# A two-layer decoder trunk on one core: three matmuls for the half-K products, column sums by ones, other homes for VectorE's work, another pace for the modulation, and the first mixer's K in blocks of 4, 6, 6

## The chip, the cores and the metric

The kernel runs on 1 core of one Trainium2 chip. Its time is device microseconds (us) of one launch; lower is better. TensorE (PE) does the matrix products, with weight loads (PEld) of their own beside them; VectorE (DVE), ScalarE (ACT) and GpSimd (POOL) do the rest; SyncE (SP) issues almost all transfers from device memory (DMA).

## The reference

The input is 256 tokens of 2048 features, in fp32. Layer 0 has a gated linear attention (GLA), layer 1 a softmax attention with forget gates (FoX); each is followed by a gated MLP (FFN) with a causal convolution of width 3. Every sub-layer's input is an RMS norm, scaled and shifted by a modulation that is computed from one conditioning vector `c`. That modulation is a matrix of 2048 by 12288 for each layer, used for a single vector.

```python
cond = jax.nn.silu(c)
for i in range(DEPTH):                      # DEPTH = 2
    mod = (cond @ w_mod[i] + b_mod[i])[:, None, :]
    sh_m, sc_m, g_m, sh_f, sc_f, g_f = jnp.split(mod, 6, axis=-1)
    h = rmsnorm(x, norm_mix[i]) * (1.0 + sc_m) + sh_m
    y = gla_mixer(h, ...) if i % 2 == 0 else fox_mixer(h, ...)
    x = x + (1.0 + g_m) * y
    h = rmsnorm(x, norm_ffn[i]) * (1.0 + sc_f) + sh_f
    x = x + (1.0 + g_f) * conv_ffn(h, ...)
return rmsnorm(x, norm_final)
...
# gla_mixer:  proj = h @ w_in  (q 1024, k 1024, v 2048, r 2048, a 16 columns), then chunked attention, @ w_out
# fox_mixer:  proj = h @ w_in  (q, k, v, og of 2048 each, 16 forget gates), softmax attention, @ w_out
# conv_ffn:   u = h @ w_up (2 x 5632 columns), conv, silu(gate) * val, @ w_down
```

## The kernel before, in words

Activations lie transposed (`xT`: features on the partitions, tokens along the free axis), so K comes in 16 tiles of 128 features. The kernel is written as a queue of work for the Tile layer, whose scheduler then sets the order of the instructions on each engine; `tc.issue_after` pins an instruction behind another.

**Products.** Each fp32 product is done with split operands: a weight tile is rounded to `wh` on ScalarE (`split_w`, line 110) and the remainder `wl` is formed on VectorE (line 111); an activation `h` or `op` is held as a high and a low part side by side. `stream_p` takes pairs of K tiles: one load `w` of 512 KB holds two K tiles of 512 columns and feeds eight (column tile, K tile) products. Each such product is a 512-column matmul of `wh` with both parts of `h` next to each other (line 554) and a 256-column one of `wl` with the high part (line 555). The two halves of the result land in different halves of a PSUM bank, and `gather` adds them while it copies them out: one ScalarE copy and one VectorE add (lines 584, 585), or two VectorE adds where an earlier sum is there (lines 582, 585). `stream_b` makes the token-major products (v, and FoX's q and k) of three 512-column matmuls, `narrow` the 16-column gates of three 256-column ones (lines 614 to 616). After every weight load's products `tick()` runs a share of the waiting background and side work.

**Blocks of K.** Products run over a part of K where the modulation for the rest isn't there yet. GLA's input products take K in `BLOCKS` of 8 and 8 tiles: all columns for the first block, then the modulation's queue is drained, then the second block adds to the first (`fold`, `run`). The first FFN does `FIRST` = 6 groups of its up product over the first 8 K tiles, drains, and then their second halves.

**Modulation.** `mod_tasks` cuts a section (`sc_m`, `sh_m`, ...) into chunks of at most 1024 columns. One task loads part of `w_mod` (`wm`) and multiplies its rows by the conditioning values, adding on VectorE into `acc` (the first row by a tensor-scalar on line 250, the others on line 252). In the start the first four K tiles go through TensorE instead (`direct`, line 246). `finish` sums `acc` over its 128 partitions: eight TensorE transposes (line 265), then eight ScalarE passes with an accumulator (line 274; in the start two VectorE reductions), then the bias. A task's load takes one of the same five ring buffers as the weight loads. `pace["bg"]` is the number of tasks per `tick()`; `set_pace(n)` spreads the tasks that wait over n ticks. Chunks marked `defer` are finished in the next `make_h`.

**Side work.** Convolutions, gates and attention steps wait in `side`, popped at `pace["side"]` per tick. In the FFN a group's four gate and four value convolutions go through it; the down product's operand `op` (`raw_operand`) is made from the activations that they write. `make_h` computes the reciprocal root of each token's mean square (`token_rstd`) and makes `h` tile by tile.

The stages in order: start (modulation of the first block, loading x and its squares), GLA input, GLA output with the first residual, FFN up and down, FoX, FoX output, second FFN.

Of the kernel before, what the change touches and what calls it, by code (L numbers as in the profile page):

```python
# [17 lines left out]
P = 128  # L18
# [22 lines left out]
BLOCKS = (8, 8)  # L41
# [14 lines left out]
N1, N2, N3, N4 = 26, 151, 152, 156  # L56
# [8 lines left out]
def kernel(  # L65
# [151 lines left out]
    def mod_tasks(l, key, f0=0, fn=D, wide=False, direct=0, defer=False):  # L217
# [8 lines left out]
        def chunk(c0, kt, st):  # L226
# [8 lines left out]
            def f():  # L235
# [5 lines left out]
                for j in range(per):  # L241
                    k = kt + j
                    col = cT[:, k:k + 1]
                    if k < direct:
                        for m in range(mn):
                            nc.tensor.matmul(st["p"][:, m:m + 1], wt[:, j, m * P:(m + 1) * P], col,
                                             start=(k == 0 and m == 0), stop=(k == direct - 1), skip_group_check=True)
# [11 lines left out]
            def finish():  # L259
                m0, mn = c0 // P, width // P  # L260
                red = tmp.tile([P, 8], F32, tag="red", name=nm("red"))
                for q0 in range(0, mn, 4):
                    pt = bank2("pt")[:, 0, :] if wide or defer else misc()
                    for m in range(min(4, mn - q0)):
                        nc.tensor.transpose(pt[:, m * P:(m + 1) * P], st["a"][:, (q0 + m) * P:(q0 + m + 1) * P],  # L265
                                            ident)
                    if wide:
                        mq = min(4, mn - q0)
                        nc.vector.tensor_reduce(out=red[:, q0:q0 + mq], in_=pt[:, :mq * P]
                                                .rearrange("p (m k) -> p m k", k=P), axis=AX.X, op=ALU.add)  # L270
                        continue
                    for m in range(min(4, mn - q0)):
                        blk = pt[:, m * P:(m + 1) * P]
                        nc.scalar.activation(blk, blk, AF.Copy, accum_out=red[:, q0 + m:q0 + m + 1])
# [140 lines left out]
    def token_rstd():  # L415
# [10 lines left out]
        for _ in range(3):  # L426
            for i in range(2):
                c1 = slice(i, i + 1)
                nc.vector.tensor_scalar(out=t[:, c1], in0=q[:, c1], scalar1=q[:, c1], scalar2=v[:, c1],
                                        op0=ALU.mult, op1=ALU.mult)  # L430
            for i in range(2):
                c1 = slice(i, i + 1)
                nc.vector.tensor_scalar(out=q[:, c1], in0=t[:, c1], scalar1=1.5, scalar2=q[:, c1],
                                        op0=ALU.subtract, op1=ALU.mult)
# [12 lines left out]
    def make_h(l, kind):  # L447
# [8 lines left out]
        def make(m):  # L456
# [8 lines left out]
            nc.scalar.activation(hi, t, AF.Identity, scale=sc, bias=sh)  # L465
            nc.vector.tensor_scalar(out=t, in0=t, scalar1=sc, scalar2=sh, op0=ALU.mult, op1=ALU.add)
# [77 lines left out]
    def stream_p(kts, c0, rhs, done=None):  # L544


        ps = [bank2().rearrange("p j (s t) -> p j s t", s=2) for _ in range(2)]
        held = []

        def mms(m, k, ws, j, hl):  # L550
            first, last = k == kts[0], k == kts[-1]
            ms = slice(j * 512 + m * P, j * 512 + (m + 1) * P)
            o = ps[m // 2][:, m % 2, :, :]
            nc.tensor.matmul(o, ws[0][:, ms], hl, start=first, stop=False, skip_group_check=True)  # L554
            nc.tensor.matmul(o[:, 0, :], ws[1][:, ms], hl[:, 0, :], start=False, stop=last, skip_group_check=True)  # L555
# [21 lines left out]
        return ps  # L577

    def gather(dst, ps, add=False):

        if add:
            nc.vector.tensor_tensor(out=dst, in0=dst, in1=ps[:, :, 1, :], op=ALU.add)
        else:
            nc.scalar.copy(out=dst, in_=ps[:, :, 1, :])  # L584
        nc.vector.tensor_tensor(out=dst, in0=dst, in1=ps[:, :, 0, :], op=ALU.add)  # L585
# [62 lines left out]
    def gla(l, h):  # L648
# [10 lines left out]
        def fold(key, ps):  # L659
# [12 lines left out]
            for b in range(4):  # L672
                dst = parts[key][:, b, :]
                if new:
                    nc.scalar.copy(out=dst, in_=ps[b // 2][:, b % 2, :])
                else:
                    nc.vector.tensor_tensor(out=dst, in0=dst, in1=ps[b // 2][:, b % 2, :], op=ALU.add)

        def run(key, kts, c0):
# [6 lines left out]
            for g in range(2):  # L686
                ps = stream_p(kts, c0 + g * 512, h)
                for b in range(2):
                    gather(parts[key][:, g * 2 + b, :].rearrange("p (j t) -> p j t", j=2), ps[b], not new)
# [210 lines left out]
    def fox(l, h):  # L900
# [43 lines left out]
        def qk_group(c0, gain, dst):  # L944
# [17 lines left out]
            def fin(hp):  # L962
                def f():
                    pt = misc().rearrange("p (j t) -> p j t", j=2)
                    for j in range(2):
                        hh = hp * 2 + j
                        for tt in range(TT):
                            blk = (tt * 2 + hh // 4) * 4 + hh % 4
                            nc.vector.tensor_scalar(out=tok4[:, blk, :], in0=tok4[:, blk, :],
                                                    scalar1=rs[:, blk:blk + 1], scalar2=None, op0=ALU.mult)  # L970
# [10 lines left out]
        def soft(hd):  # L981
            def f():
# [9 lines left out]
                nc.vector.tensor_scalar(out=s[:, 0:P], in0=p_[:, 0:P], scalar1=cumt[:, 0, hd:hd + 1],  # L992
                                        scalar2=None, op0=ALU.add)
# [310 lines left out]
```

## Time and profile before

| | |
|---|---|
| median of 3 runs | 2592.15 us (2590.53 to 2594.13) |
| profiled execution | 2593.84 us; its span 2592.1 us |
| granted TensorE clock, mean | 0.975 |
| read from device memory | 633.14 MB, 245 GB/s over the span |
| transfers of `w_mod` | 352 of 512 KB, 16 of 1024 KB |

A span is the time from the first instruction to the last. A group's row names line, engine and operation, output and inputs, shapes and count, then total busy time and mean ns of one, then the engine's idle time before and what ended it. A row of the timeline gives start and length. A row of the waits names who waited for whom: us in total, times, longest.

### The profile page before, as it was taken

The page shows a single profiled execution, that of the slowest core. Times are in us where ns is not written, and L with a number is a line of the kernel's source. Part 1 is how long each engine was busy: PE and PEld are TensorE (multiplying, and loading weights), DVE is VectorE, ACT ScalarE, POOL GpSimd, SP SyncE. Part 2 cuts the span into 40 slices and gives each one's busy share as a digit, 9 for nine tenths or more (in the row PEclk, how much of TensorE's full clock was granted, in tenths as well). Part 3 has the DMA queues.
Part 4 walks back from the last instruction along what each step waited for, and adds up shares of the span by engine and source line. Part 5 has one row for each costly group of instructions (what it writes and reads, how often), then busy time and mean ns, then how long its engine had stood idle before and what let it go on. Part 6 is the DMA issues. An engine that isn't in the chain of part 4 may idle for free.

```text
span 2592.1 us, 36814 instructions
## 1 busy us (share of the span) xinstructions
PE 2486.6 (96%) x13738; PEld 2139.2 (83%) x13738; DVE 2010.2 (78%) x2784; ACT 1288.2 (50%) x1964; POOL 18.1 (1%) x35
## 2 busy tenths in 40 slices
PE   6999998899999999899999999999899999999998
PEld 6887887788888888788888888778788888888887
DVE  7877988888789999877587888877877777767554
ACT  2447353445555565443454555543655555565332
POOL 0000000000000000000000000100000000000000
PEclk7999998899999999999999999999999999999999
DMA  8896877789567888898589988768577777765653
GB/s 335 276 311 218 294 235 255 247 293 324 178 186 259 295 295 295 269 305 299 178 267 307 305 269 229 215 228 267 171 221 229 226 224 225 223 196 195 191 189 116
DMA packets 267727, 637.67 MB, mean 246 GB/s; under 512 B 23449, under 2 KB 24459, under 8 KB 267164
## 3 DMA queue, kind: packets, MB, share of 16 engines
q1 hardware_dynamic: 267160, 635.17, 75.3%
q8 instruction: 108, 1.77, 0.3%
q14 instruction: 71, 0.58, 0.1%
q10 hardware_dynamic: 388, 0.15, 0.0%
HBM read 633.14 MB, written 2.10 MB: 245 GB/s over the span
## 4 chain that ended last, share of the span: by engine, by line
PE 72%; DVE 12%; DMA 10%; issue 3%; ACT 3%; DVEq 0%; SPq 0%; ACTq 0%
PE pa L554 38%; PE pa L555 19%; DMA wm<-in_w_mod_dram 7%; DVE wl L111 4%; PE pa L601 4%; PE pa L599 4%; PE pa L600 4%; DVE acc L252 3%; ACT wh L110 1%; DVE xT L624 1%; DMA w<-in_ffn_w_down_dram 1%; DMA w<-in_gla_w_in_dram 1%; DMA w<-in_ffn_w_up_dram 0%; PE pm L411 0%; PE pm L265 0%
## 5 line engine op out<-in xcount | busy, mean ns | idle before, releaser
L110 ACT CAST wh<-w 128x1024 fp32r<-128x1024 f32 x819 | 856.2, 1049 | 986.5 <-PE pa L554 429.5
L111 DVE TENSOR_TENSOR wl<-w,wh 128x1024 fp32r<-128x1024 f32 x819 | 994.4, 1218 | 368.0 <-ACT wh L110 361.4
L554 PE MATMUL pa<-h,wh 128*128 128x512 f32 x3584 | 1264.4, 399 | 15.9 <-DVE h L467 7.8
L555 PE MATMUL pa<-h,wl 128*128 128x256 f32 x3584 | 992.8, 282 | 6.7 <-DVE wl L111 6.6
L554 PEld LDWEIGHTS pa<-h,wh 128*128 128x128 f32 x3584 | 671.4, 189 | 169.3 <-ACT h L465 8.1
L555 PEld LDWEIGHTS pa<-h,wl 128*128 128x128 f32 x3584 | 681.9, 190 | 21.9 <-DVE wl L111 9.4
L554 PE MATMUL pa<-op,wh 128*128 128x512 f32 x1920 | 676.0, 398 | 18.9 <-DVE op L483 14.8
L555 PE MATMUL pa<-op,wl 128*128 128x256 f32 x1920 | 531.9, 281 | 4.2 <-DVE wl L111 4.2
L252 DVE SCALAR_TENSOR_TENSOR acc<-wm,cT,acc 128x1024 f32<-128x1024 f32 x352 | 450.7, 1280 | 104.9 <-DMA wm<-in_w_mod_dram 103.9
L554 PEld LDWEIGHTS pa<-op,wh 128*128 128x128 f32 x1920 | 359.8, 189 | 103.6 <-DVE op L483 15.2
L555 PEld LDWEIGHTS pa<-op,wl 128*128 128x128 f32 x1920 | 363.9, 190 | 9.5 <-DVE wl L111 6.0
L600 PE MATMUL pa<-wh,h 128*128 128x512 f32 x512 | 201.6, 394 | 0.0
L599 PE MATMUL pa<-wh,h 128*128 128x512 f32 x512 | 200.7, 393 | 0.0
L601 PE MATMUL pa<-wl,h 128*128 128x512 f32 x512 | 197.5, 394 | 0.1
L1081 ACT ACTIVATE y<-u,cw 128x256 f32<-128x256 f32 x176 | 99.0, 597 | 37.3 <-DVE u L585 22.0
L601 PEld LDWEIGHTS pa<-wl,h 128*128 128x128 f32 x512 | 96.5, 189 | 20.1 <-DVE wl L111 0.4
L599 PEld LDWEIGHTS pa<-wh,h 128*128 128x128 f32 x512 | 96.6, 189 | 19.3
L600 PEld LDWEIGHTS pa<-wh,h 128*128 128x128 f32 x512 | 96.5, 189 | 19.2
L1082 DVE SCALAR_TENSOR_TENSOR y<-u,cw,y 128x255 f32<-128x255 f32 x176 | 84.0, 477 | 0.0
L1084 DVE SCALAR_TENSOR_TENSOR y<-u,cw,y 128x254 f32<-128x254 f32 x176 | 82.6, 476 | 0.7
L585 DVE TENSOR_TENSOR u<-u,pa 128x512 f32<-128x512 f32 x112 | 75.7, 679 | 4.0 <-ACT u L584 3.9
L624 DVE SCALAR_TENSOR_TENSOR xT<-pa,mod,xT 128x256 f32<-128x256 f32 x128 | 53.1, 476 | 20.1 <-PE pa L555 20.1
(238 smaller groups left out, 1249.4 us busy)
## 6 DMA issues: line engine op xcount, KB each, us to landing
wm<-in_w_mod_dram SPq DMA_DIRECT2D x352, 512.0 KB, 5.1
w<-in_ffn_w_up_dram SPq DMA_DIRECT2D x352, 512.0 KB, 4.7
w<-in_ffn_w_down_dram SPq DMA_DIRECT2D x176, 512.0 KB, 5.1
w<-in_fox_w_in_dram SPq DMA_DIRECT2D x128, 512.0 KB, 5.3
w<-in_gla_w_in_dram SPq DMA_DIRECT2D x96, 512.0 KB, 4.9
wm<-in_w_mod_dram SPq DMA_DIRECT2D x16, 1024.0 KB, 12.3
w<-in_gla_w_out_dram SPq DMA_DIRECT2D x32, 512.0 KB, 5.5
w<-in_fox_w_out_dram SPq DMA_DIRECT2D x32, 512.0 KB, 5.6
```

The lines of the kernel that those rows point to most:

```text
L110: nc.scalar.copy(out=hi, in_=src)
L111: order["v"] = nc.vector.tensor_tensor(out=lo, in0=src, in1=hi.bitcast(F32), op=ALU.subtract).ins
L252: nc.vector.scalar_tensor_tensor(out=st["a"], in0=wt[:, j, :], scalar=col, in1=st["a"], op0=ALU.mult, op1=ALU.add)
L554: nc.tensor.matmul(o, ws[0][:, ms], hl, start=first, stop=False, skip_group_check=True)
L555: nc.tensor.matmul(o[:, 0, :], ws[1][:, ms], hl[:, 0, :], start=False, stop=last, skip_group_check=True)
L599: nc.tensor.matmul(o, lh[:, ts_], wh[:, hs_], start=first, stop=False)
L600: nc.tensor.matmul(o, ll[:, ts_], wh[:, hs_], start=False, stop=False)
L601: nc.tensor.matmul(o, lh[:, ts_], wl[:, hs_], start=False, stop=last)
L624: nc.vector.scalar_tensor_tensor(out=xT[:, m, :], in0=ps[:, j, s_, :], scalar=modcol(l, key, m), in1=xT[:, m, :], op0=ALU.mult, op1=ALU.add)
L1081: nc.scalar.activation(y, u, AF.Identity, scale=cw[:, l * 3 + 2, r:r + 1], bias=cw[:, 6 + l, r:r + 1])
L1082: nc.vector.scalar_tensor_tensor(out=y[:, 1:], in0=u[:, :T - 1], scalar=cw[:, l * 3 + 1, r:r + 1], in1=y[:, 1:], op0=ALU.mult, op1=ALU.add)
L1084: nc.vector.scalar_tensor_tensor(out=y[:, 2:], in0=u[:, :T - 2], scalar=cw[:, l * 3, r:r + 1], in1=y[:, 2:], op0=ALU.mult, op1=ALU.add)
```

## The change

- **Half-K products.** `stream_p(wide=False)`, used for GLA's q, k and r and for the first FFN's half-K groups, does each product in three 256-column matmuls into the same PSUM half (high by high, high by low, low by high), in one two-bank buffer instead of two. The fold is one 1024-element copy or add.
- **Column sums.** `finish` multiplies 128-column pieces of `acc` by a column of ones, straight into PSUM (into the buffer of the direct products where these exist), and one VectorE operation adds the bias. The transposes, ScalarE passes and reductions go.
- **ScalarE.** The first row of an accumulation, the scaling of FoX's q and k, the softmax's bias and its scaling, and for m >= 2 the making of `h` move from VectorE to ScalarE.
- **Newton steps.** `token_rstd` does three operations on both columns instead of four on single ones, three times.
- **Pace.** In the first FFN the remaining up groups run 0.3 tasks per tick (before: the queue spread over 151 ticks from there); at the down product the rest is spread over 80 ticks, and the side pace becomes 1.
- **Blocks.** `BLOCKS` is (4, 6, 6). The start's modulation chunks have 512 columns, four K tiles to a 1 MB load; those of the two later blocks 768 columns, one K tile to a load of 384 KB (393 KB in thousands).

```diff
-BLOCKS = (8, 8)
+BLOCKS = (4, 6, 6)
...
-N1, N2, N3, N4 = 26, 151, 152, 156
+UPRATE = 0.3
+N1, N2, N3, N4 = 26, 80, 152, 156
...
                     elif k == direct:
-                        nc.vector.tensor_scalar(out=st["a"], in0=wt[:, j, :], scalar1=col, scalar2=None, op0=ALU.mult)
+                        nc.scalar.activation(st["a"], wt[:, j, :], AF.Copy, scale=col)
...
             def finish():
-                red = tmp.tile([P, 8], F32, tag="red", name=nm("red"))
-                for q0 in range(0, mn, 4):
-                    ...                          # transposes, then ScalarE passes or a VectorE reduction
+                pt = st["p"] if direct else bank2("pt")[:, 0, :] if wide or defer else misc()
+                for m in range(mn):
+                    nc.tensor.matmul(pt[:, m:m + 1], st["a"][:, m * P:(m + 1) * P], one,
+                                     start=(m == 0 and not direct), stop=True, skip_group_check=True)
-                nc.vector.tensor_tensor(out=dst, in0=red[:, :mn], in1=bm[:, b0:b0 + mn], op=ALU.add)
-                if direct:
-                    nc.vector.tensor_tensor(out=dst, in0=dst, in1=st["p"][:, :mn], op=ALU.add)
+                nc.vector.tensor_tensor(out=dst, in0=pt[:, :mn], in1=bm[:, b0:b0 + mn], op=ALU.add)
...
         for _ in range(3):                       # token_rstd
-            for i in range(2):
-                ...
+            nc.vector.tensor_tensor(out=t, in0=q, in1=q, op=ALU.mult)
+            nc.vector.tensor_tensor(out=t, in0=t, in1=v, op=ALU.mult)
+            nc.vector.scalar_tensor_tensor(out=q, in0=t, scalar=1.5, in1=q, op0=ALU.subtract, op1=ALU.mult)
...
-            nc.scalar.activation(hi, t, AF.Identity, scale=sc, bias=sh)
-            nc.vector.tensor_scalar(out=t, in0=t, scalar1=sc, scalar2=sh, op0=ALU.mult, op1=ALU.add)
+            if m < 2:
+                ...                              # as before
+            else:
+                nc.scalar.activation(t, t, AF.Identity, scale=sc, bias=sh)
+                nc.scalar.copy(out=hi, in_=t)
...
+            o = ps[0][:, m // 2, m % 2, :]       # stream_p, wide=False
+            nc.tensor.matmul(o, ws[0][:, ms], hl[:, 0, :], start=(first and m % 2 == 0), stop=False,
+                             skip_group_check=True)
+            nc.tensor.matmul(o, ws[0][:, ms], hl[:, 1, :], start=False, stop=False, skip_group_check=True)
+            nc.tensor.matmul(o, ws[1][:, ms], hl[:, 0, :], start=False, stop=last, skip_group_check=True)
...
+        def take(dst, ps, new):                  # GLA's folds
+            if new:
+                nc.scalar.copy(out=dst, in_=ps)
+            else:
+                nc.vector.tensor_tensor(out=dst, in0=dst, in1=ps, op=ALU.add)
...
-                            nc.vector.tensor_scalar(out=tok4[:, blk, :], in0=tok4[:, blk, :],
-                                                    scalar1=rs[:, blk:blk + 1], scalar2=None, op0=ALU.mult)
+                            nc.scalar.activation(tok4[:, blk, :], tok4[:, blk, :], AF.Copy, scale=rs[:, blk:blk + 1])
...
-                nc.vector.tensor_scalar(out=s[:, 0:P], in0=p_[:, 0:P], scalar1=cumt[:, 0, hd:hd + 1],
-                                        scalar2=None, op0=ALU.add)
+                nc.scalar.activation(s[:, 0:P], p_[:, 0:P], AF.Identity, bias=cumt[:, 0, hd:hd + 1])
...                                              # likewise the other half, and both scalings by 1/sum
-    ffn(0, lazy(make_h(0, "f"), KT, 2, (8,)), (ALL[:8], between, lambda: set_pace(N2)))
+    def after():
+        pace["bg"] = UPRATE
+    def down():                                  # called ahead of the down product
+        pace["side"] = 1.0
+        set_pace(N2)
+    ffn(0, lazy(make_h(0, "f"), KT, 2, (8,)), (ALL[:8], between, after), down)
```

The order of the instructions moves with it. In the start, TensorE's queue before the change goes from the small row transposes straight to the transposes of x (`xtok`; `rows` and `brow` are small parameters):

```order
L159 MATMUL pm_103<-ident,rows_92 128x98
L179 MATMUL pm_120<-ident,brow_118 128x96
L179 MATMUL pm_125<-ident,brow_123 128x96
L384 MATMUL pm_157<-ident,xtok_153 128x128
L384 MATMUL pm_157<-ident,xtok_155 128x128
```

The same place after the change, where `wm_256` is the fifth load of the modulation, the first of the shift's:

```order
L160 MATMUL pm_103<-ident,rows_92 128x98
L264 MATMUL pd_136<-ones,acc_258 128x1 x4
L180 MATMUL pm_120<-ident,brow_118 128x96
L247 MATMUL pd_283<-cT,wm_256 128x1 x9
L180 MATMUL pm_125<-ident,brow_123 128x96
L373 MATMUL pm_157<-ident,xtok_153 128x128
L373 MATMUL pm_157<-ident,xtok_155 128x128
```

The first column sum and nine products of that load now stand ahead of x. SP's queue in GLA's first block, before (`w` are weight loads, `wm` modulation loads):

```order
L231 DMA wm_635<-in_w_mod_dram 128x1024
L520 DMA w_638<-in_gla_w_in_dram 128x2x512
L231 DMA wm_660<-in_w_mod_dram 128x1024
L520 DMA w_667<-in_gla_w_in_dram 128x2x512
L520 DMA w_703<-in_gla_w_in_dram 128x2x512
L520 DMA w_726<-in_gla_w_in_dram 128x2x512
L231 DMA wm_748<-in_w_mod_dram 128x1024
```

and after:

```order
L232 DMA wm_601<-in_w_mod_dram 128x768
L514 DMA w_606<-in_gla_w_in_dram 128x1024
L232 DMA wm_636<-in_w_mod_dram 128x768
L232 DMA wm_639<-in_w_mod_dram 128x768
L514 DMA w_642<-in_gla_w_in_dram 128x1024
L232 DMA wm_672<-in_w_mod_dram 128x768
L514 DMA w_678<-in_gla_w_in_dram 128x1024
L232 DMA wm_696<-in_w_mod_dram 128x768
L232 DMA wm_699<-in_w_mod_dram 128x768
```

The modulation's loads, narrower now, outnumber the weights'. SP's queue in the middle of the first FFN's down product, before:

```order
L520 DMA w_10067<-in_ffn_w_down_dram 128x2x512
L520 DMA w_10090<-in_ffn_w_down_dram 128x2x512
L231 DMA wm_10112<-in_w_mod_dram 128x1024
L520 DMA w_10114<-in_ffn_w_down_dram 128x2x512
L520 DMA w_10137<-in_ffn_w_down_dram 128x2x512
L231 DMA wm_10159<-in_w_mod_dram 128x1024
L520 DMA w_10162<-in_ffn_w_down_dram 128x2x512
```

and after:

```order
L508 DMA w_11081<-in_ffn_w_down_dram 128x2x512
L232 DMA wm_11103<-in_w_mod_dram 128x1024
L508 DMA w_11106<-in_ffn_w_down_dram 128x2x512
L232 DMA wm_11128<-in_w_mod_dram 128x1024
L508 DMA w_11131<-in_ffn_w_down_dram 128x2x512
L232 DMA wm_11153<-in_w_mod_dram 128x1024
L508 DMA w_11156<-in_ffn_w_down_dram 128x2x512
```

Two modulation loads for three of weights have become one for one. In the whole product 73 of its modulation tasks stand where 48 stood, in the last up groups 22 where 48 stood, and in GLA's output 38 where 28 stood.

More of the change, by code (lines that the diff above doesn't have):

```diff
@@ L576, in stream_p, with gather @@
                     done(m // 2, ps[m // 2])
[L577 to L584, printed above, removed]
+        return ps if wide else ps[0]
+    def gather(dst, ps):
+        nc.scalar.copy(out=dst, in_=ps[:, :, 1, :])
         nc.vector.tensor_tensor(out=dst, in0=dst, in1=ps[:, :, 0, :], op=ALU.add)
@@ L671, in fold @@
                 parts[key] = bigt([P, 4, 512], key)
[L672 to L677, printed above, removed]
+            for tt in range(TT):
+                take(parts[key][:, 2 * tt:2 * tt + 2, :], ps[tt], new)
         def run(key, kts, c0):
```

65 lines of the change are left out of this document (28 added, 37 removed).

## The prediction

> **What bounds the kernel now.** I read the page first, then busy times cut where each weight matrix's first product starts, then single rows of TensorE, then the waits at the seams.
>
> ```profile
> PE 2486.6 (96%) x13738; PEld 2139.2 (83%) x13738; DVE 2010.2 (78%) x2784; ACT 1288.2 (50%) x1964; POOL 18.1 (1%) x35
> ```
>
> TensorE is busy almost throughout, so work taken from another engine pays only where TensorE waits. In the table the columns are length, PE, PEld, DVE, ACT and POOL busy, granted clock, DMA share, GB/s. In order: start, GLA input block 0, block 1 with the attention, GLA output; first FFN: half-K groups, their second halves, remaining up groups, down; FoX input, its gate with the rest of the attention, FoX output; second FFN up, down.
>
> ```profile
> 0.00:62.00 62.00, 41.07 (x193) 38.56 (x193) 43.63 (x76) 15.89 (x27) 1.18 (x9) 0.77 0.89 350
> 62.00:213.00 151.00, 141.76 (x745) 120.09 (x745) 116.40 (x130) 69.85 (x112) 0.00 (x0) 0.97 0.85 284
> 213.00:391.00 178.00, 173.00 (x1034) 147.67 (x1035) 155.94 (x226) 97.77 (x156) 4.32 (x10) 0.97 0.75 246
> 391.00:514.00 123.00, 103.95 (x572) 89.13 (x571) 102.81 (x145) 48.19 (x83) 0.00 (x0) 0.91 0.77 259
> 514.00:660.00 146.00, 139.17 (x787) 120.46 (x785) 123.36 (x140) 71.83 (x114) 0.00 (x0) 0.98 0.88 300
> 660.00:796.00 136.00, 135.89 (x765) 118.51 (x766) 113.95 (x178) 74.46 (x99) 0.00 (x0) 0.98 0.59 176
> 796.00:1025.00 229.00, 228.14 (x1308) 198.70 (x1307) 217.03 (x296) 134.41 (x212) 0.00 (x0) 1.00 0.87 294
> 1025.00:1294.00 269.00, 257.08 (x1462) 223.94 (x1462) 196.60 (x229) 119.94 (x186) 0.00 (x0) 0.97 0.79 266
> 1294.00:1589.00 295.00, 294.87 (x1353) 241.69 (x1354) 242.47 (x374) 151.81 (x250) 4.30 (x8) 0.99 0.87 280
> 1589.00:1718.00 129.00, 122.00 (x677) 101.95 (x676) 98.36 (x190) 67.32 (x133) 8.27 (x8) 0.97 0.74 203
> 1718.00:1824.00 106.00, 98.24 (x560) 84.08 (x558) 81.31 (x115) 46.87 (x76) 0.00 (x0) 0.98 0.75 250
> 1824.00:2325.00 501.00, 498.08 (x2834) 433.34 (x2835) 373.80 (x515) 281.60 (x407) 0.00 (x0) 0.99 0.70 219
> ```
>
> A busy PE is not a full one, so the price of a product comes from starts. Line 554 starts a 512-column product, 555 a 256-column one; lines 614 to 616 (`narrow`) are three 256-column ones, the very pattern that the change gives to half-K products.
>
> ```profile
> 84.12 0.40 PE L554 MATMUL pa<-h,wh 128*128 128x512 f32 x1
> 90.36 0.40 PE L554 MATMUL pa<-h,wh 128*128 128x512 f32 x1
> 90.71 0.28 PE L614 MATMUL pm<-h,wh 128*128 128x256 f32 x1
> 92.82 0.27 PE L614 MATMUL pm<-h,wh 128*128 128x256 f32 x1
> ```
>
> 18 pairs in 6.24 us are 0.3467 us each; 6 triples in 2.11 us, 0.3517. A 512 KB weight load feeds 8 pairs, 2.77 us. So the first FFN's down product needs 88 x 2.77 = 244 of its 269 us, its last up groups 80 x 2.77 = 222 of 229, GLA's output 89 of 123.
>
> **Three matmuls.** 512 products of GLA (q, k, r) and 768 of the first FFN change: 1280 x 0.005 = +6.4 us. If no third weight load were hidden it would be 1280 x 0.156 (PEld busy over its count) = +200 us, but `narrow`, with three loads a triple, hides it; below zero is excluded, since the columns streamed are the same. The Trainium skill, "TensorE: Matmul & The Clock Gate", Back-to-back issue gap, gives 518 and 262 cycles, so 780 against 786; an estimate by that page is +3.2 us. The rows differ by twice that, and I keep theirs. The folds of these products shrink from two VectorE passes to one:
>
> ```profile
> L585 DVE TENSOR_TENSOR u<-u,pa 128x512 f32<-128x512 f32 x112 | 75.7, 679 | 4.0 <-ACT u L584 3.9
> L252 DVE SCALAR_TENSOR_TENSOR acc<-wm,cT,acc 128x1024 f32<-128x1024 f32 x352 | 450.7, 1280 | 104.9 <-DMA wm<-in_w_mod_dram 103.9
> L274 ACT ACTIVATE pm<-pm 128x128 f32<-128x128 f32 x144 | 37.5, 261 | 3.9 <-PE pm L265 3.1
> L969 DVE TENSOR_SCALAR tok<-tok,qrs 128x128 f32<-128x128 f32 x64 | 13.6, 279 | 0.1
> ```
>
> 72 of the 136 `u` adds go for 12 wide ones: 49 less 15 us of VectorE, hidden under TensorE's 135.89 of 136 us, so nothing.
>
> **The start.** The first block needs 8 modulation loads of 1 MB, not 16.
>
> ```profile
> 6.72 13.81 PE L246 MATMUL pd<-cT,wm 128*128 128x1 f32 x64 [3.93 <-DVE cT L166]
> 22.10 1.28 DVE L252 SCALAR_TENSOR_TENSOR acc<-wm,cT,acc 128x1024 f32<-128x1024 f32 x1 [0.78 <-DMA wm<-in_w_mod_dram]
> 31.02 1.18 ACT L398 ACTIVATE sq<-xT 128x512 f32<-128x512 f32 x2
> 36.93 1.71 PE L411 MATMUL pm<-ones,ss 128*128 128x1 f32 x8
> 38.68 0.16 DVE L420 TENSOR_SCALAR tv<-pm 128x2 f32<-128x2 f32 x1 [0.21 <-PE pm L411]
> 38.87 0.17 DVE L422 TENSOR_SCALAR tq<-tv 128x2 int32<-128x2 int32 x1
> 61.99 0.76 PE L554 MATMUL pa<-h,wh 128*128 128x512 f32 x1 [2.81 <-ACT h L465]
> ```
>
> Eight loads and the two of x are 10.5 MB, 30 us at the start's 350 GB/s; last accumulation at about 35. But x then decides: its transposes stand behind nine column products on the fifth load (landed 22.1, nine at 13.81/64 = 0.216: 24.0, against 21.3 before), so the squares end at 34.9 instead of 32.2; add 0.7, eight sums 1.7, twelve small VectorE steps at 0.2 (38.68 to 38.87), broadcast and h 3.3: first product at 43 instead of 62: **-19** (-22 if modulation decided alone, -8 if the chain is as interleaved as now, where it ran from 38.68 to 47).
>
> **Where that work goes.** The other 32 loads move into GLA. Block 0 carries 32 loads of 393 KB and 25 of weights, 25.7 MB, in the time of four K tiles (32 triples, 24 products of 0.229 and `narrow`'s 0.35: 17.1 us each, 68 us), so 375 GB/s wanted. What can be had is the dispute:
>
> ```profile
> 440.00:470.00 30.00, 27.87 (x162) 24.11 (x161) 25.91 (x31) 13.01 (x27) 0.00 (x0) 1.00 0.90 306
> 560.00:600.00 40.00, 40.00 (x235) 35.11 (x234) 33.47 (x33) 21.85 (x39) 0.00 (x0) 1.00 0.93 322
> ```
>
> At 322 GB/s TensorE lost nothing; at 306, modulation and weights one for one through the same ring of five buffers, it starved. 322 at share 0.93 would be 346 at a full share; I take 334, between. Block 0: 77 us, **+8** (+5 at 350, +16 at 306). Block 1, 32 MB in six tiles' 103 us, wants 311: **+1**. A third block means a second seam; now TensorE waits 4.1 us there, and runs slowly after:
>
> ```profile
> PE pm L614 <- ACT h L465: 4.1, 1, 4.1
> PE pa L554 <- DVE h L467: 4.3, 1, 4.3
> PE pa L554 <- DVE op L483: 7.3, 1, 7.3
> 1819.44 3.40 ACT pt L274 x24
> ```
>
> The first row is that seam; two cheaper ones of 4 or so for one of 5: **+3**. In GLA's output 38 modulation loads stand in place of 28: 5.2 MB, 16 us at 334; the stretch's DMA share is 0.77, so I let not quite half vanish: **+9** (0 to +17). The last input block and the output have less on VectorE and ScalarE, the norm before 514 too: **-4** (0 to -8).
>
> **Column sums by ones.** 176 ScalarE passes (0.26 us) with their accumulator reads go; 192 one-column products replace as many transposes, no dearer on TensorE. It matters at seams: second row above (the FFN's K halves) **-3**; last row, ScalarE between the FoX output and the second FFN, **-4**; the like at 1284, **-3**. The shorter Newton steps are in these.
>
> **Pacing.** The last up groups carry 22 modulation loads, not 48: 26 x 1.28 = 33 us less VectorE in a stretch where it is busy 217 of 229: **-4** of the 7 us lost. Then the third row: TensorE waits 7.3 us for an operand whose gated activations queue behind modulation and its ScalarE passes. One side task a tick from the down product on, fewer loads ahead and no passes remove it: **-9** with the slow clock behind it. What is late next is the down product itself: 73 modulation loads now stand among about 85 weight loads, 82.8 MB in 236 us, 351 GB/s wanted. VectorE, 197 of 269, has room for 25 x 1.28 = 32 us. At 334 it takes 248: **+12** (0 at 350, +35 at 306).
>
> **ScalarE.** FoX's scalings leave VectorE, 64 of them at 0.279; ScalarE's price lies near its 0.261 row. Under 294.87 of 295 us: nothing. In the stretch from 1589 TensorE waits, VectorE is the busier: **-3** (-7 to +5, if ScalarE's queue grows late). h made through ScalarE: nothing; it is asked for two tiles ahead. Rest: **-1**.
>
> Sum: 6.4 - 19 + 8 + 1 + 3 + 9 - 4 - 3 - 4 - 3 - 4 - 9 + 12 - 3 - 1 = -10.6. The profiled execution took 2593.84 (span 2592.1 and 1.74), 1.7 over the median of 2592.15, so on the median I forecast **2582 us**.
>
> **The rivals.**
> *The copies keep up.* If 350 GB/s of the start holds in mixed stretches, down costs 0, output 0, block 0 +5: 24 less, and I add 6 for starved clocks that vanish: 2552 to 2558. For it: 350 at share 0.89. Against: that was in 1 MB loads with a deep buffer. The Trainium skill, "DMA: Bandwidth & Descriptors", Specifications, puts a core's HBM limit near 358 GB/s; by that limit all but block 0 would keep up. The 306 and 322 rows stay below it, and neither shows a transfer-free bound, so it stays a rival.
> *The modulation queue becomes the bound* (slower). At 306 GB/s one for one, the rate at which the output product starved: down +35, output +17, block 0 +16, block 1 +2: 40 more, 2622. The forecast's gain is gone below about 327 GB/s, and slower by 0.2% begins near 323. For it: three stretches now have the one-for-one order that starved. Against: there residual adds shared the blame.
> *The start gives little.* If x's chain stays interleaved, -8 in place of -19: 2593, no change.
>
> **How the numbers follow.** Forecast 0.42 (own range 2572 to 2591), copies keep up 0.14, queue bound 0.24, little start 0.20. A measurement tells about 0.2%, 5 us, from no change. Faster: 0.37 of the first, 0.14, and 0.01; same: 0.05, 0.13 and 0.02; slower: 0.22 and 0.06. Range 2556 to 2612: it leaves out the ends of the second and third case.
>
> **What would show it.** Right: first heavy product near 43 us; triples of 0.352; no wait over 2 us at the up-to-down seam; the down product's share of DMA above 0.9, longer than 244 us but under 260. Wrong: down over 270 us or output over 140 (queue bound); first product after 50 us; ScalarE passing 90% in FoX's gate.

## The result and the profile after

The changed kernel takes **2652.01 us** (median of 4 runs, 2646.24 to 2653.47) against 2591.81 for the kernel before in the same runs: a ratio of 1.0228, 95% interval 1.0212 to 1.0244. It is 2.3% slower, where 2582 was forecast; the time lies outside the range. The profiled execution took 2646.24 us, its span 2644.5, against a span of 2592.1 before: 52.4 us to explain.

Busy times of the changed kernel, from its page:

```profile
PE 2530.6 (96%) x15146; PEld 2228.1 (84%) x15146; DVE 1928.9 (73%) x2499; ACT 1316.5 (50%) x1799; POOL 14.2 (1%) x35
```

VectorE did get 81 us lighter (2010.2 to 1928.9), as the change intends. TensorE's share is the same 96% of a longer span. The share says nothing here; the stages do. The windows of the changed kernel, cut at the same events as those of before (columns as there), now with three blocks of GLA's input; the FoX gate and output are rows 11 and 12, and the last row, as in the table of before, is the second FFN's up product:

```profile
0.00:47.00 47.00, 27.51 (x128) 25.52 (x128) 26.86 (x60) 16.32 (x26) 1.18 (x9) 0.92 0.79 288
47.00:142.00 95.00, 80.93 (x516) 73.35 (x516) 65.86 (x78) 41.97 (x50) 0.00 (x0) 0.90 0.85 271
142.00:267.00 125.00, 115.48 (x764) 106.63 (x765) 90.07 (x103) 45.57 (x58) 0.00 (x0) 0.93 0.80 249
267.00:414.00 147.00, 136.44 (x1042) 123.62 (x1040) 120.28 (x150) 80.47 (x109) 4.26 (x10) 0.98 0.76 245
414.00:548.00 134.00, 114.61 (x601) 95.08 (x601) 107.21 (x154) 44.92 (x52) 0.00 (x0) 0.91 0.78 252
548.00:695.00 147.00, 145.54 (x1191) 144.55 (x1192) 104.98 (x112) 71.31 (x85) 0.00 (x0) 0.96 0.85 290
695.00:830.00 135.00, 135.00 (x1149) 135.00 (x1148) 104.93 (x139) 78.25 (x106) 0.00 (x0) 1.00 0.67 195
830.00:1056.00 226.00, 226.00 (x1299) 197.89 (x1298) 185.12 (x258) 131.16 (x180) 0.00 (x0) 1.00 0.74 236
1056.00:1347.00 291.00, 272.09 (x1521) 233.79 (x1519) 224.04 (x253) 115.53 (x129) 0.00 (x0) 0.97 0.84 289
1347.00:1650.00 303.00, 302.88 (x1378) 244.22 (x1379) 222.04 (x294) 176.04 (x296) 4.98 (x8) 0.99 0.76 272
1650.00:1770.00 120.00, 119.12 (x688) 101.81 (x688) 84.34 (x123) 81.48 (x166) 3.78 (x8) 1.00 0.71 222
1770.00:1875.00 105.00, 100.85 (x571) 88.17 (x569) 79.45 (x111) 43.38 (x50) 0.00 (x0) 0.96 0.74 248
1875.00:2378.00 503.00, 501.26 (x2851) 437.28 (x2852) 369.50 (x498) 282.26 (x383) 0.00 (x0) 1.00 0.69 219
```

GLA's output begins 23.6 us later than before (414.3 for 390.7) although GLA's input begins 14.6 us earlier: the input takes 366.8 us for 328.7. The output takes 133.7 for 123.3, the first FFN's up product 508.4 for 511.1, its down product 290.5 for 268.7, FoX 528.5 for 530.6, the second FFN and the end 1.4 more. So two places carry it all: GLA up to the FFN, +34, and the first down product, +22.

In the down product these are the two longest waits of the changed kernel and TensorE's own longest, 1090 to 1260 us, the stretch without seams:

```profile
ACT wh L111 <- DMA w<-in_ffn_w_down_dram: 80.8, 44, 3.7
DVE wl L112 <- ACT wh L111: 34.5, 34, 2.7
PE pa L545 <- DVE wl L112: 4.6, 5, 2.5
```

TensorE waits for `wl`, `wl` for `wh`, `wh` for the weight load. Why the load is late shows in the chain of waits there, 1176 to 1191 us (start, length, what; small steps left out):

```profile
1176.51 6.14 DMA w<-in_ffn_w_down_dram
...
1182.74 1.06 ACT wh L111
...
1183.82 1.24 DVE wl L112
1185.08 5.59 DMA w<-in_ffn_w_down_dram
```

GLA's first block has such a chain too:

```profile
102.62 4.87 DMA wm<-in_w_mod_dram
...
107.58 0.09 DVE acc L253
107.66 0.85 issue
108.51 1.23 DVE wl L112
109.76 4.77 DMA wm<-in_w_mod_dram
```

It is a loop: a load lands, the engines get to it in their queues (ScalarE and VectorE split weights, VectorE adds up modulation), which frees a ring buffer, and only then does the next load start. The turns shown take 8.6 us in the down product and 7.1 us in the block, of which 6.1 and 4.9 are landing; the block's turns between 95 and 125 us lie between 6.9 and 8.0. Five buffers of 393 and 524 KB, 459 on the average, in 7.1 us give 323 GB/s at best, five of 524 KB in 8.6 us 305; these are estimates from the rows, beside 271 measured in the block and 322 in the down product. If they are right, the rate is held down by the ring and not by the transfers, and that is put to the test below.

### The profile page after: what moved, and what is told of

Same layout as the page of the kernel before. It is cut to its first block, busy times and chain, and to the rows that moved or that the text cites. A ratio compares the mean times of both kernels' runs of the same rounds, so it can differ in the third digit from the quotient of the medians.

```text
span 2644.5 us, 39187 instructions
## 1 busy us (share of the span) xinstructions
PE 2530.6 (96%) x15146; PEld 2228.1 (84%) x15146; DVE 1928.9 (73%) x2499; ACT 1316.5 (50%) x1799; POOL 14.2 (1%) x35
## 4 chain that ended last, share of the span: by engine, by line
PE 71%; DMA 13%; DVE 10%; issue 3%; ACT 2%; DVEq 0%; SPq 0%; ACTq 0%
PE pa L544 28%; PE pa L545 14%; DMA wm<-in_w_mod_dram 7%; DVE wl L112 4%; PE pa L550 4%; PE pa L594 4%; PE pa L551 4%; PE pa L548 4%; PE pa L592 4%; PE pa L593 4%; DMA w<-in_ffn_w_down_dram 4%; DVE acc L253 3%; ACT wh L111 1%; DMA w<-in_gla_w_out_dram 1%; DVE xT L617 1%
## 5 line engine op out<-in xcount | busy, mean ns | idle before, releaser
L544 PE MATMUL pa<-h,wh 128*128 128x512 f32 x2304 | 811.5, 396 | 3.8 <-DVE h L455 3.4
L545 PE MATMUL pa<-h,wl 128*128 128x256 f32 x2304 | 642.0, 282 | 0.0
L253 DVE SCALAR_TENSOR_TENSOR acc<-wm,cT,acc 128x1024 f32<-128x1024 f32 (+2 forms) x382 | 462.2, 1210 | 135.1 <-DMA wm<-in_w_mod_dram 125.3
L545 PE MATMUL pa<-op,wl 128*128 128x256 f32 x1920 | 527.6, 284 | 14.6 <-DVE wl L112 14.3
L544 PEld LDWEIGHTS pa<-h,wh 128*128 128x128 f32 x2304 | 430.8, 188 | 102.1 <-ACT rb L444 2.4
L544 PEld LDWEIGHTS pa<-op,wh 128*128 128x128 f32 x1920 | 356.8, 190 | 97.5 <-DVE op L471 10.9
L548 PE MATMUL pa<-h,wh 128*128 128x256 f32 x1280 | 364.2, 285 | 6.6 <-ACT h L454 4.0
L551 PE MATMUL pa<-h,wl 128*128 128x256 f32 x1280 | 363.9, 285 | 6.7 <-DVE wl L112 6.7
L550 PE MATMUL pa<-h,wh 128*128 128x256 f32 x1280 | 364.0, 285 | 0.9 <-DVE h L455 0.8
L548 PEld LDWEIGHTS pa<-h,wh 128*128 128x128 f32 x1280 | 246.3, 193 | 9.3 <-ACT h L454 4.1
L550 PEld LDWEIGHTS pa<-h,wh 128*128 128x128 f32 x1280 | 245.8, 192 | 1.9 <-DVE h L455 1.8
L592 PE MATMUL pa<-wh,h 128*128 128x512 f32 x512 | 204.6, 401 | 0.8 <-ACT wh L111 0.6
L593 PE MATMUL pa<-wh,h 128*128 128x512 f32 x512 | 204.3, 399 | 0.0
L592 PEld LDWEIGHTS pa<-wh,h 128*128 128x128 f32 x512 | 96.8, 189 | 24.0 <-ACT wh L111 1.7
```

The lines of the kernel that those rows point to most:

```text
L253: nc.vector.scalar_tensor_tensor(out=st["a"], in0=wt[:, j, :], scalar=col, in1=st["a"], op0=ALU.mult, op1=ALU.add)
L548: nc.tensor.matmul(o, ws[0][:, ms], hl[:, 0, :], start=(first and m % 2 == 0), stop=False, skip_group_check=True)
L550: nc.tensor.matmul(o, ws[0][:, ms], hl[:, 1, :], start=False, stop=False, skip_group_check=True)
L551: nc.tensor.matmul(o, ws[1][:, ms], hl[:, 0, :], start=False, stop=last, skip_group_check=True)
L592: nc.tensor.matmul(o, lh[:, ts_], wh[:, hs_], start=first, stop=False)
L593: nc.tensor.matmul(o, ll[:, ts_], wh[:, hs_], start=False, stop=False)
```

## The experiments

Two theories came first. **L**: there are too many modulation loads beside each weight load, and the loop sets the time; the blocks and the pace are to blame. **E**: the edits on the engines (triples, column sums, work on ScalarE) lengthened something. Four kernels undo or do one part alone.

```diff
 e1_blocks_88 (after)     -BLOCKS = (4, 6, 6)           +BLOCKS = (8, 8)
 e2_pace_old (after)      -N2 = 80; pace["bg"] = UPRATE; pace["side"] = 1.0
                          +N2 = 151; set_pace(N2) after the half-K groups, as before
 e3_both_old (after)      both of these
 e4_before_466 (before)   -BLOCKS = (8, 8)              +BLOCKS = (4, 6, 6)
```

> The changed kernel with K in blocks of 8 and 8 again, all else as changed. Theory L (the loop of loads: time went where modulation loads stand more than about 0.75 to one weight load, so in GLA's two short first blocks, its output and the down product): GLA from the first product to the end of the output goes back from 501 to about 452 us plus 3 for the triples, the start from 47 to 62, the rest stays: 2652 - 49 + 3 + 15 = 2621 us, plus or minus 6. Theory E (the edits on the engines, three matmuls and ScalarE, slowed it): blocks matter only through the start, 2652 + 15 = 2667 us.

> The changed kernel with the old pace of the modulation in the first FFN (the queue spread over 151 ticks from the last up groups on, side pace 0.7), blocks 4, 6, 6. Theory L: the down product with its norm goes back from 290 to 269 us or less, less if the column sums shorten the seam; the last up groups go from 226 to 229: 2652 - 18 = 2634 us, plus or minus 5. Theory E: the down product stays near 290, 2652 us.

> Blocks 8 and 8 and the old pace; three matmuls, column sums by ones, ScalarE's share and the short Newton steps stay. Theory L: about 2652 - 31 - 18 = 2603 us at most; by the sum of the prediction for these edits alone (+6 triples, -3 -3 -4 at seams, -4 and -3 for lighter engines) 2581 to 2592. Theory E: 2630 us or more.

> The kernel before with blocks of 4, 6, 6 and nothing else. Theory L: GLA loses here as it does in the changed kernel: start -15, input +38, output +10: 2592 + 33 = 2625 us, plus or minus 8. Theory E: the start's gain stays, 2577 us.

The stages that differ, in us, of these and the later kernels. "First product" and "output begins" are times from the start of the span (the second is the start and GLA's input together); "output" (GLA's) and "down" (the first) are lengths, from the first product to the next stage's. These come from the profiled execution, the total is a median; its ratio is to the kernel before in the same runs, where that took between 2591.8 and 2596.0 us:

| kernel | first product | output begins | output | down | total (ratio) |
|---|---|---|---|---|---|
| before | 62.0 | 390.7 | 123.3 | 268.7 | 2591.81 |
| after | 47.4 | 414.3 | 133.7 | 290.5 | 2652.01 (1.0228) |
| e1: 8-8 | 61.7 | 389.8 | 118.3 | 289.2 | 2607.65 (1.0045, 1.003 to 1.006) |
| e2: old pace | 47.5 | 415.4 | 133.8 | 272.3 | 2637.06 (1.0153, 1.0136 to 1.017) |
| e3: both | 62.0 | 389.9 | 116.8 | 271.1 | 2593.98 (0.9998, 0.9988 to 1.0008) |
| e4: before, 4-6-6 | 48.1 | 418.2 | 134.2 | 269.2 | 2631.72 (1.0137, 1.0122 to 1.0152) |
| m1: thin sum | 47.5 | 391.9 | 127.7 | 281.0 | 2604.96 (one run) |
| m2: no loads | 47.3 | 375.7 | 118.5 | 269.8 | 2565.90 (one run) |
| m3: six buffers | 47.4 | 403.8 | 127.5 | 269.9 | 2610.48 (one run) |
| m5: half the bytes | 47.6 | 380.6 | 122.9 | 271.9 | 2576.30 (one run) |
| c1: e3, six buffers | 61.7 | 387.2 | 108.0 | 271.6 | 2585.67 (0.9953, 0.9938 to 0.9968) |
| c4: e1, six buffers | 61.6 | 386.1 | 108.6 | 274.8 | 2583.83 (0.9960, 0.9944 to 0.9976) |
| c5: before, six buffers | 61.9 | 392.9 | 126.1 | 269.6 | 2591.73 (0.9993, 0.9984 to 1.0001) |
| c7: 4-4-8, six buffers | 47.4 | 403.7 | 110.6 | 276.3 | 2598.20 (1.0021, 1.001 to 1.0031) |

Within the same runs the blocks cost 43 us (e2 less e3; 36 when put into the kernel before) and the pace 14 (e1 less e3). After itself ran beside a kernel before that was 4 us faster, so the same steps counted from it (after less e1, after less e2) are 44 to 49 and 15 to 19 us. e2 and e4 came out as L has it, and e1 some 7 us below its range. With both undone, the time is that of before: with five buffers all edits on the engines together are worth nothing measurable, where the sum had promised 2581 to 2592. E falls. What in the loop of L sets its length was then asked four ways, each on the changed kernel.

```diff
 m1_thin_sum      a ring load's accumulation  -acc[:, :1024]   +acc[:, :8]
 m2_no_loads      -wm from device memory      +a constant tile, same VectorE work
 m3_ring_six      -RING = 5; T2 = 5; SB = 4   +RING = 6; T2 = 4; SB = 3
 m5_half_bytes    m1, and  -dma_start(wm)     +dma_start(wm[:, :, :width // 2])
                  (in m2 and m5 the first row of a ring load's sum, on ScalarE, reads the constant tile too)
```

> The kernel after, with the modulation's accumulation on VectorE cut to 8 columns per load for the loads that go through the ring (it leaves out most of the modulation's sum; every load, buffer and queue position stays; some 310 operations of 1.28 us become some 0.1 us). In after GLA's input took 366.8 us, its output 133.7, the first down product 290.5. Theory B (bytes: the transfers' rate is the limit): these stay within 6 us each. Theory V (VectorE's time is the loop): input near 325, output near 110, down near 265, total some 80 us less. Theory R (round trip of five buffers: issue, landing of 5 us, turn in VectorE's queue, next issue): the trip of 7.1 us loses its 1.28, so the starved stretches shorten by at most 18%: input 340 to 350, down 272 to 280, total 30 to 50 us less.

> The kernel after without the modulation's loads outside the start (the accumulation reads a constant tile in their place, with the same operations on VectorE; it leaves out those bytes and their turns in the ring). Theories B and R: input at 285 or less, output near 95, down at 250 or less, total at least 90 us less, near 2545. Theory V: input still above 350, down above 280, total above 2630.

> The kernel after with six ring buffers in place of five (to make room T2 = 4 and SB = 3, two pools of small tiles). Bytes, order and VectorE's work stay. Theory B: input 366, output 134, down 290, each within 6 us. Theory R: six buffers per round trip give up to a fifth more loads per us where TensorE starves: input 335 to 350, down 268 to 280. Theory V: as B.

> As the thin sum, and each modulation load through the ring brings only the first half of its columns: same number of loads, buffers and turns, half the modulation's bytes (it leaves out half of those bytes and most of the sum). Theory B: input near 285, output near 95, down near 250, as if there were hardly a load. Theory R: a load of half the size lands hardly sooner (384 KB took 4.9 us, 512 KB 5.2), so within 15 us of the thin sum in total. Theory V: as the thin sum within 5 us.

The middle of the down product, 1090 to 1260 us, in the changed kernel and then in m1, m3, m5 and m2 (columns as above):

```profile
1090.00:1260.00 170.00, 164.15 (x926) 140.09 (x925) 132.68 (x129) 63.45 (x63) 0.00 (x0) 0.99 0.93 322
```

```profile
1090.00:1260.00 170.00, 168.05 (x965) 145.73 (x963) 88.89 (x138) 65.63 (x65) 0.00 (x0) 1.00 0.96 336
```

```profile
1090.00:1260.00 170.00, 170.00 (x992) 149.29 (x991) 143.60 (x144) 68.99 (x68) 0.00 (x0) 1.00 0.97 350
```

```profile
1090.00:1260.00 170.00, 170.00 (x980) 148.84 (x979) 88.20 (x131) 65.10 (x64) 0.00 (x0) 1.00 0.79 254
```

```profile
1090.00:1260.00 170.00, 168.37 (x979) 147.78 (x977) 132.61 (x133) 64.85 (x65) 0.00 (x0) 1.00 0.53 174
```

The rows are the same times and not quite the same part of the product: m3's begins 16 us earlier, and the stretch that lies as far behind its start (1074 to 1244) has 170.00 us of TensorE and 344 GB/s.

The third row decides the down product. With one buffer more, the same bytes and VectorE work and nearly the same order (the kernel's look-ahead is the ring less one, so a weight load is asked for one turn earlier), TensorE is busy for all of the 170 us, and the transfers run at 350 GB/s: the stage falls from 290.5 to 269.9, to what it takes with no modulation load at all (269.8). So 322 was never the transfers' limit, and bytes as the bound (theory B) are out there; the round trip (theory R) holds, within its range of 268 to 280. The other rows show what the trip is made of. VectorE's 1.28 us is part of it: m1 recovers nearly half of the down product's loss, and its 344.4 us of input, 281.0 of down (272 to 280 expected) and 41 us in all are nearly R's numbers. Theory V, VectorE's time alone, had asked for 265 there and for no gain in m3, and is out in this stage. That bytes don't matter to R was wrong: m5 is 29 us shorter than m1, where at most 15 were expected. A smaller load does land sooner, with less traffic around it. These are issue-to-landing medians, of after and then of m5:

```profile
wm<-in_w_mod_dram SPq DMA_DIRECT2D x320, 512.0 KB, 5.2
wm<-in_w_mod_dram SPq DMA_DIRECT2D x64, 384.0 KB, 4.9
```

```profile
wm<-in_w_mod_dram SPq DMA_DIRECT2D x320, 256.0 KB, 4.0
wm<-in_w_mod_dram SPq DMA_DIRECT2D x64, 192.0 KB, 3.7
```

Half the bytes took about three quarters of the time.

The input is less clear-cut. Six buffers give back 10.4 us of it, where 17 to 32 were expected, so R holds there only in part. m2 missed all of its numbers: without loads, the input still takes 328.4 us, the output 118.5 and the down product 269.8, where at most 285, near 95 and at most 250 were expected. The loads cost 80 us in all (2646 to 2566); what stays is not loads. In the last of the three input blocks it is in part VectorE's work: the block takes 147.5 us in after, 145.3 with six buffers, 144.5 without loads, but 136.3 with the thin sum.

The rest shows in the output product. These are its groups on TensorE of after, of m2 and of c4 (blocks 8-8, described below): the 512-column products, and the broadcasts of the attention's normalisation with those of the FFN's norm (line 358; 367 in m2):

```profile
L544 PE MATMUL pa<-op,wh 128*128 128x512 f32 x256 | 95.8, 416 | 11.0 <-DVE op L471 5.9 <-ACT wh L111 4.2 <-DVE xT L617 0.9
L358 PE MATMUL pm<-dg,ones 128*128 128x128 f32 x12 | 2.9, 348 | 3.6 <-DVE dg L356 3.6
```

```profile
L553 PE MATMUL pa<-op,wh 128*128 128x512 f32 x256 | 95.1, 412 | 7.4 <-DVE op L480 6.8 <-DVE xT L626 0.6
L367 PE MATMUL pm<-dg,ones 128*128 128x128 f32 x12 | 2.7, 339 | 2.8 <-DVE dg L365 2.8
```

```profile
L544 PE MATMUL pa<-op,wh 128*128 128x512 f32 x256 | 89.3, 396 | 4.7 <-DVE op L471 3.4 <-DVE xT L617 1.4
L358 PE MATMUL pm<-dg,ones 128*128 128x128 f32 x4 | 1.5, 470 | 2.8 <-DVE dg L356 2.8
```

The whole output of c4 as a window:

```profile
386.10:494.70 108.60, 99.82 (x578) 87.14 (x576) 96.08 (x128) 44.08 (x50) 0.00 (x0) 0.96 0.87 294
```

Twelve broadcasts, eight of them the attention's, run in the output where the last block has six K tiles; only four, the norm's, where the same code has eight tiles. TensorE waits there for `op`, and its products are slower (416 and 412 ns for 396, at a granted clock of 0.91 after, 0.92 in m2 and 0.96 in c4). m2 has no loads and shows it as well. So a second theory, **T**: the attention's side work doesn't fit under a block of six K tiles, and its tail runs in the output product. In the kernel before it didn't quite fit under eight either; its output has the twelve too:

```profile
L369 PE MATMUL pm<-dg,ones 128*128 128x128 f32 x12 | 3.4, 389 | 6.2 <-DVE dg L367 6.2
```

With eight tiles the edits on the engines had thus brought the tail under the block (e1 and e3 have four broadcasts in the output, and it takes 118.3 and 116.8), and the shorter block pushed it out again.

Four kernels test R and T in the total, all with six buffers (T2 = 4, SB = 3):

```diff
 c1_old_order_ring6 (e3)    -RING = 5   +RING = 6
 c4_new_pace_ring6 (e1)     -RING = 5   +RING = 6
 c5_before_ring6 (before)   -RING = 5   +RING = 6
 c7_blocks_448_ring6 (m3)   -BLOCKS = (4, 6, 6)   +BLOCKS = (4, 4, 8)
```

> The kernel after with both orders undone (blocks 8 and 8, the old pace: 2593.98 us with five buffers) and six ring buffers. If the round trip of the buffers limits (theory R, as the six-buffer run of the kernel after bore out in the down product, 290.5 to 269.9), the places with modulation gain a little here too: GLA's input 327.9 to some 320, its output 116.8 to some 111, the down product 271 to 269; 2578 to 2586 in all. If the old order had enough buffers: 2592 to 2596.

> The kernel after with blocks 8 and 8 (2607.65 us with five buffers) and six ring buffers; the new pace stays. Theory R: the down product falls from 289.2 to 270, GLA's output from 118.3 to some 112, its input from 328 to some 321: 2576 to 2586, so that the new pace costs nothing against the old one. Bytes as the limit: 2600 to 2608.

> The kernel before with six ring buffers and nothing else (T2 = 4 and SB = 3 make room). Theory R: GLA's input 328.7 to some 321, its output 123 to some 117, the down product 268.7 unchanged (it had slack): 2576 to 2586. If the ring was no limit in the old order: 2590 to 2595. If the smaller pools of tiles cost something in FoX's gate, that stage shows it: over 131 us in place of 129.5.

> The kernel after with blocks 4, 4, 8 and six ring buffers (4, 6, 6 with six: 2610.48 us; 8, 8 with six and the new pace: 2583.83). The start stays at 47. Theory T (the attention's side work, some 42 us of TensorE, doesn't fit under a last block of six K tiles, and its tail runs in the output product): the last block takes 173 to 176 and the output 108 to 112, with 4 of the broadcast products of line 358 in the output where six tiles left 12. Theory R for the blocks ahead: block 0 with 16 loads some 78, block 1 with 32 loads in four tiles some 90, as long as the first block of 4, 6, 6. So the FFN begins near 498 and the whole takes 2582 to 2594. Without T the output stays near 127, the FFN begins near 520 and the whole takes 2600 to 2612.

c4 came out as R has it in the total, from 1.0045 with five buffers to 0.9960 with six, the output 118.3 to 108.6; the down product fell from 289.2 to 274.8, not to 270. c1's total is in R's range too, though its gain is almost all in the output (116.8 to 108.0) and the down product gained nothing (271.1 and 271.6). c5 did not: with the kernel before, six buffers are worth 0.07%, and the interval includes no change. Its down product has 48 modulation loads, not 73, and gains nothing (269.6); its output (126.1) still has the tail's twelve broadcasts, and that these hold it is likely but not shown. c1 beside c5 shows something else: with six buffers the edits on the engines are worth 0.4% (0.9953 and 0.9993, intervals apart), where with five they were worth nothing; the output takes 108.0 for 126.1, and the first FFN's up product gives a part of it back, 517.2 for 505.6. The smaller pools of tiles cost nothing that shows: FoX's gate took 126.7 us in place of 129.5.

c7 bears T out in the stages: its output begins when m3's did (403.7 and 403.8) and takes 110.6 us in place of 127.5, with four broadcasts of line 358:

```profile
L544 PE MATMUL pa<-op,wh 128*128 128x512 f32 x256 | 91.0, 401 | 1.3 <-DVE op L471 0.7 <-DVE xT L617 0.6
L358 PE MATMUL pm<-dg,ones 128*128 128x128 f32 x4 | 1.5, 470 | 2.8 <-DVE dg L356 2.8
```

It has fewer modulation loads in the output too, 26 for m3's 34, so the 17 us between them are not the tail's alone. m2, with no loads but the tail, takes 118.5 for c4's 108.6, with 26 loads and no tail: the tail costs at least 10 us, and at most about 17.

In the total T's range of 2582 to 2594 was missed: the blocks ahead took 81.6 and 97.5 us, not 78 and 90. The start's 14 us are spent again on loads under a starving TensorE, its FFN begins at 514.3 (c4: 494.7), and in all, at 2598.20, it is 0.2% slower than before.

c1 and c4 beat the kernel before by 0.4 to 0.5%; their intervals overlap, so which of the two is better isn't told. Left open: with 4-6-6, the first block takes 88 to 90 us in m1, m3 and m5 alike and 76.4 without loads. Neither VectorE's time alone (m1), nor the buffer (m3), nor VectorE's time with half the bytes (m5) freed it; the buffer together with either was not tried.

## Why the prediction was wrong

**The step that failed** is "322 at share 0.93 would be 346 at a full share; I take 334, between", and every term that was a demand divided by it. It took a rate read in a stretch as a capacity of the transfers. In the down product the runs showed that the rate came from a ring of five buffers and its round trip: with a sixth the same loads ran at 350 GB/s and the stage at 269.9 us for 290.5. The trip is longer when the added loads each need a turn in VectorE's queue (281.0 with the thin sum). In GLA the same loads cost 38 us of the input and 15 of the output (after less m2), of which the sixth buffer gives back 10 and 6, the thin sum 22 and 6, and the thin sum with half the bytes 34 and 11; how these add up is open.

- *Block 0, +8*: with 68.4 us of products as its base it took 94.8, so +26. The blocks' 271 and 249 GB/s lie below 306, the lowest rate that I had allowed.
- *Block 1, +1*: it took 124.5 for 102.6 of products, +22. This was the clearest miss: a demand of 311 below the supposed capacity of 334 was taken to be free. Without loads the two blocks stood at +8.0 and +4.8 (seams), so the loads cost 18 and 17.
- *Down, +12*: +21.8. m3 shows the price at six buffers: +1.2 over before, at the 350 GB/s for which the text had written 0. The sign "under 260" didn't follow from the sum: 268.7 with its -9, -3 and +12 is 269.
- *Output, +9 and -4 for lighter engines*: +10.4, the two nearer +5, for a partly wrong reason. Without loads it is still 118.5, and 10 to 17 us of the stage are T's, a step that the prediction didn't have at all. The kernel before had the tail too, so the tail is no part of the +10.4; it is why the lighter engines, which took the output to 118.3 under eight tiles (e1), gave nothing here. The prediction counted the attention's stretch as lighter, where that had lost two K tiles of cover.
- *Third seam, +3*: the blocks without loads leave 12.8 us over products for the seams and the clock of two blocks; I can't divide it further.
- *Start, -19*: -14.6, between the two ends. x's transposes were held up by more than the nine products foreseen. TensorE in the start of the changed kernel:

```profile
23.74 3.12 PE L247 MATMUL pd<-cT,wm 128*128 128x1 f32 x14
...
26.92 1.06 PE L373 MATMUL pm<-ident,xtok 128*128 128x128 f32 x4
27.78 2.98 PE L247 MATMUL pd<-cT,wm 128*128 128x1 f32 x14
30.62 4.87 PE L373 MATMUL pm<-ident,xtok 128*128 128x128 f32 x20
...
40.41 1.86 PE L400 MATMUL pm<-ones,ss 128*128 128x1 f32 x8 [2.46 <-DVE ss L393]
...
47.44 0.58 PE L548 MATMUL pa<-h,wh 128*128 128x256 f32 x1 [1.15 <-ACT h L450]
```

  They begin behind fourteen column products, at 26.9 (24.0 in the prediction), and fourteen more cut in; the sums start at 40.4, not 35.6. From there to the first product it is 7.0 us, where 1.7 + 2.4 + 3.3 = 7.4 were counted.
- *Triples, +6.4*: three starts apart they are 0.353 us (0.3517 in the prediction's row). Beside the prediction's 0.3467 for a pair, from one stretch of 18, that is +8.5 over 1280 products; beside 0.350, the median of the 384 pairs in the second halves of before, +4. The half-K groups' second halves, which TensorE bounds alone, show that it didn't lengthen them: they took 135.7 us, all of it 384 triples of 0.353, where before they took 136.4 with 4.3 us of waits in them.
- *Up groups, -4*: -2.6. *The up-to-down seam, -9*: the wait for `op` fell from 7.3 to 3.1 us, so -4, and "no wait over 2 us" was not reached:

```profile
PE pa L544 <- DVE op L471: 3.1, 1, 3.1
```

- *FoX gate, -3*: its stage lost 10.3 us and the one ahead of it gained 8.4, -1.9 together; two of the attention's steps ran in the earlier stage, and how the rest divides is open. ScalarE was busy 81.48 of 120 us there, far from the 90% named.
- *The edits on the engines* as a whole: the sum had +6.4 - 4 - 3 - 4 - 3 - 3 - 1, some -12; with five buffers e3 measured nothing (0.9998).

**The rivals.** The direction was the second rival's, "the modulation queue becomes the bound", given 0.24: its place and sign were right. Its price of 40 us fell short of the 70 by which the forecast missed, because it too priced loads as bytes (306 GB/s) and block 1 at +2. "The copies keep up" fell with five buffers and holds with six in the down product. The Trainium skill, "DMA: Bandwidth & Descriptors", Specifications, has the limit near 358 GB/s per core; its section Measured has 425 for 16 MB and a core that streams alone. The trace agrees with the second: 20 to 30 us in the start of the kernel before, 412 GB/s with 1 MB loads (a share over 1 comes from counting a transfer where it starts; from 10 to 47 us the rate is 406 to 412):

```profile
20.00:30.00 10.00, 7.60 (x38) 5.59 (x38) 8.35 (x12) 6.36 (x12) 0.00 (x0) 1.00 1.04 412
```

So the 350 of the whole start was a mean with a slow first and last part (289 GB/s up to 10 us, 247 from 47 us on), and neither it nor 358 was a ceiling. Of the signs named beforehand, "down over 270" came true; "output over 140" and "first product after 50" did not.

## What to carry to other kernels

A rate read off a stretch is not a capacity until one knows what holds it: count the buffers and the length of one round trip (issue, landing, the turn in the consumer's queue), and take buffers by size over trip as the ceiling. If a change adds loads to a shared ring, price its turns and not only its bytes, and test it with one buffer more before trading start-up time for loads under the products. A block that is made shorter also loses cover for the side work that ran under it; look where that work's last step goes.

## What was unexpected

A DMA share of 0.93 looked full and was not: the down product ran at 0.97 and 350 GB/s with one more buffer. In GLA's output the loss was larger than the waits: after has 19 us of idle TensorE and c4 9 us (134.0 less 114.6, 108.6 less 99.8), yet the stage takes 25 us longer. The difference is slower products, at a granted clock of 0.91 for 0.96, and the few moved ones; whether the waits bring the slower clock wasn't tested.
